# A planner's cost table for TensorE set to other numbers

## The chip, the cores and the metric

The kernel runs on one core of one Trainium2 chip. The metric is the device time of one execution in microseconds (us); smaller is better. The engines are named as in the profile: PE is TensorE (matrix products and transposes), DVE is VectorE, ACT is ScalarE, POOL is GpSimd, SP is the engine that here issues all transfers (DMA). PEclk is the share of TensorE's full clock of 2.4 GHz that was granted; 0.5 is its lower level, 1.2 GHz.

## What is computed

One layer of a hybrid encoder on two request groups that share the weights: 528 rows of a new stream (16 meta rows and 512 frames) and 64 rows of a running one. Cut to what matters:

```
h = rms_norm(x, pre_gain)                       # 592 rows of 2048
g_q, g_k, g_v, g_z, g_r, s_q, s_k, s_v, s_z, m_gla, m_sb = split(h @ w_in)
log_a = log_sigmoid(g_r @ w_a2 + b_a) / 16      # decays
o_gla, s_new = gla_recurrence(g_q, g_k, g_v, log_a, s0)        # 4 heads, key width 128, value width 256
y_gla = (rms_norm(o_gla) * silu(g_z)) @ w_up_gla
o_sb  = stick_breaking_attention(s_q, s_k, s_v)                # 8 heads of 128, with 1024 cached keys
y_sb  = (o_sb * silu(s_z)) @ w_up_sb
y = x + rms_norm((sigmoid(m_gla) * y_gla + sigmoid(m_sb) * y_sb) @ w_o, post_gain)
```

## The kernel before

**The products.** All large products are done at about full fp32 precision with three products each: weights and activations are split into a high and a low part, and `passes` runs high times high, high times low and low times high. The weight product is also cut by one level of Strassen's scheme (`strassen`): a column block of 256 is a *pair* of 14 *units*, which use the seven operand blocks W11, W22, S3, S1, S2, W12 and S4 in this order, two units each. A unit is four 128x128 weight blocks, so twelve products on PE, of 288 or 296 columns each. The operand tiles of these blocks are called `h0h`, `h0l` (W11) to `h6h`, `h6l`; S1 is `h3`, S3 `h5` and S4 `h2`. There are 44 such pairs for `w_in`, then the units of the two up projections, the linear rest and `w_o`, 786 in all.

**What a unit needs.** SP loads the weights into `raw` (three buffers). DVE forms the sums S1 to S4 in place (`raw<-raw`). ACT casts a quarter of `raw` to the high part `whi`, DVE subtracts to get the low part `wlo`. `whi` and `wlo` are rings of four tiles, and `convert` (from line 322) starts a unit only when the unit four places earlier has been done on PE. When S2 is done, DVE adds its bank to `u` twice (`u<-u,b`), and the second sum uses the bank of S1. S4 is accumulated onto the bank of S1, so its first unit must wait for these adds; its products are `b<-h2h,whi`.

**The side work.** Beside the units run the decays (a scan whose results `nu` go out as `d_cs`), four heads of the gated recurrence (`gla_head`: loads of `k`, `cs` and `q`; products of `q` and `k`; four levels in which DVE, ACT and POOL make `x` from `cs`, `q` and `k` and PE multiplies it into a bank that DVE copies by a mask into `sc`; turned values `cs<-b`; state products `b<-cs,k`) and eight stick-breaking heads (with the sums `L` on POOL).

**What sets the order.** Each of these is a Python generator. `Plan.run` repeatedly takes the stream whose next step is due first, and it emits that step; so the program text, and with it the order on every in-order engine and on SP, comes out of the plan's own clock. `Plan.note` advances this clock: an instruction begins when its engine is free and its inputs are ready, and lasts for what `Plan.cost` says. Nothing in the table is seen by the chip. All instructions go through one helper, so that every row of the profile shows line L197; the rows are told apart by their tiles.

Of the kernel before, what the change touches and what calls it, by code (L numbers as in the profile page):

```python
# [9 lines left out]
F32 = mybir.dt.float32  # L10
# [68 lines left out]
class Plan:  # L79
# [19 lines left out]
    def cost(self, eng, name, out, ins, summed):  # L99
        n = 1  # L100
        for x in out.shape[1:]:
            n *= x
        psum = any(x.tensor.name in self.psum for x in ins)
        if eng == "pe":
            dt = ins[0].dtype
            if dt == BF16:
                return 0.107
            if name == "transpose":
                return 0.053 if n < 64 else 0.11
            return max(0.214, n * 1.67e-3) if dt == F32 else max(0.11, n * 0.42e-3) + 0.003  # L110
        if eng == "act":
            return (0.055 if psum else 0.095) + (0.09 if summed or len(ins) > 1 else 0.0) + n * 0.83e-3
        if eng == "dve":
            if name == "tensor_scalar" and not psum:
                return 0.07 + n * 0.52e-3
            return 0.07 + n * (6.3e-3 if name == "reciprocal" else 1.04e-3)
        if name == "memset":
            return 0.04 + n * 0.83e-3
        return 0.15 + n * (3.5e-3 if name == "tensor_scalar" else 2.1e-3)
# [1854 lines left out]
```

## Time and profile before

| | |
|---|---|
| median of 3 runs | 1744.12 us (1739.87 to 1744.42) |
| profiled execution | 1741.68 us, of it 1739.9 us span |
| mean granted TensorE clock | 0.986 |
| PE, DVE, ACT, POOL busy | 96%, 72%, 49%, 10% of the span |
| instructions in the span | 31534, of them 12089 products on PE |

The busy shares are averages over the whole span: the stretch up to 700 us has the decays and the recurrence as side work, the one up to about 1100 us the stick-breaking heads, and the rest is almost products alone. A row of the timeline gives the start, the duration and, in brackets, how long the engine had been idle and what released it. Products overlap in the pipeline, so that each is listed as longer than the distance between two starts.

### The profile page before, as it was taken

The page shows a single profiled execution, that of the slowest core. Times are in us where ns is not written, and L with a number is a line of the kernel's source. Part 1 is how long each engine was busy: PE and PEld are TensorE (multiplying, and loading weights), DVE is VectorE, ACT ScalarE, POOL GpSimd, SP SyncE. Part 2 cuts the span into 40 slices and gives each one's busy share as a digit, 9 for nine tenths or more (in the row PEclk, how much of TensorE's full clock was granted, in tenths as well). Part 3 has the DMA queues.
Part 4 walks back from the last instruction along what each step waited for, and adds up shares of the span by engine and source line. Part 5 has one row for each costly group of instructions (what it writes and reads, how often), then busy time and mean ns, then how long its engine had stood idle before and what let it go on. Part 6 is the DMA issues. An engine that isn't in the chain of part 4 may idle for free.

```text
span 1739.9 us, 31534 instructions
## 1 busy us (share of the span) xinstructions
PE 1670.2 (96%) x12089; PEld 1610.1 (93%) x12089; DVE 1250.6 (72%) x2081; ACT 853.8 (49%) x1759; POOL 182.2 (10%) x293
## 2 busy tenths in 40 slices
PE   4998999899999999999999999999999999999997
PEld 2798999889999998999999999999999999999996
DVE  5877878887987886886677667666766435687777
ACT  5554444344454353455565555555544323355554
POOL 2100220120130021021020011111000000000000
PEclk9999999999999999999999999999999999999998
DMA  7144234344444424455445544554447444423336
GB/s 189 37 140 131 77 107 139 101 116 123 122 117 128 132 60 119 126 163 159 133 137 152 148 140 117 158 158 126 128 138 218 143 142 124 122 79 103 104 80 218
DMA packets 323904, 224.14 MB, mean 129 GB/s; under 512 B 17436, under 2 KB 293432, under 8 KB 322584
## 3 DMA queue, kind: packets, MB, share of 16 engines
q1 hardware_dynamic: 323016, 219.49, 44.3%
q10 hardware_dynamic: 736, 2.62, 0.4%
q8 instruction: 95, 1.56, 0.4%
q14 instruction: 57, 0.47, 0.1%
HBM read 179.17 MB, written 42.90 MB: 128 GB/s over the span
## 4 chain that ended last, share of the span: by engine, by line
PE 89%; DVE 5%; DMA 2%; ACT 1%; issue 1%; POOL 1%; SPq 0%; DVEq 0%; ACTq 0%; POOLq 0%
PE b L197 89%; DVE wlo L197 2%; DVE raw L197 1%; DMA xt<-in_x_sample 1%; ACT whi L197 0%; DVE u L197 0%; DVE t L197 0%; DMA q<-d_gq 0%; POOL h5l L197 0%; DMA xt<-in_x_prompt 0%; DVE x L197 0%; POOL L L197 0%; DVE out L197 0%; SPq L197 0%; DMA raw<-in_w_in 0%
## 5 line engine op out<-in xcount | busy, mean ns | idle before, releaser
L197 ACT CAST whi<-raw 128x512 fp32r<-128x512 f32 x786 | 482.0, 620 | 627.6 <-PE b L197 516.2
L197 DVE TENSOR_TENSOR wlo<-raw,whi 128x512 fp32r<-128x512 f32 x786 | 552.6, 713 | 303.9 <-ACT whi L197 293.7
L197 DVE TENSOR_TENSOR raw<-raw 128x1024 f32<-128x1024 f32 (+1 forms) x232 | 259.5, 1121 | 6.0
L197 PE MATMUL b<-m,whi 128*128 128x288 f32 x912 | 183.5, 296 | 0.0
L197 PEld LDWEIGHTS b<-m,whi 128*128 128x128 f32 x912 | 146.1, 188 | 0.0
L197 PE MATMUL b<-h0h,whi 128*128 128x288 f32 (+1 forms) x480 | 134.3, 304 | 1.3 <-ACT whi L197 1.3
L197 PE MATMUL b<-m,wlo 128*128 128x288 f32 x456 | 134.2, 294 | 0.0
L197 PE MATMUL b<-h6h,whi 128*128 128x288 f32 (+1 forms) x480 | 133.8, 303 | 0.0
L197 PE MATMUL b<-h6l,whi 128*128 128x288 f32 (+1 forms) x480 | 131.5, 298 | 1.9 <-DVE h6l L197 1.8
L197 PE MATMUL b<-h4h,whi 128*128 128x288 f32 (+1 forms) x480 | 133.0, 302 | 0.0
L197 PE MATMUL b<-h1h,whi 128*128 128x288 f32 (+1 forms) x480 | 132.1, 300 | 0.0
L197 PE MATMUL b<-h0l,whi 128*128 128x288 f32 (+1 forms) x480 | 131.5, 299 | 0.0
L197 PE MATMUL b<-h4l,whi 128*128 128x288 f32 (+1 forms) x480 | 130.4, 296 | 0.0
L197 PE MATMUL b<-h1l,whi 128*128 128x288 f32 (+1 forms) x480 | 130.3, 296 | 0.0
L197 PE MATMUL b<-h0h,wlo 128*128 128x288 f32 (+1 forms) x416 | 124.4, 299 | 1.5 <-DVE wlo L197 1.5
L197 PE MATMUL b<-h4h,wlo 128*128 128x288 f32 (+1 forms) x416 | 123.2, 296 | 1.6 <-DVE wlo L197 1.6
L197 PE MATMUL b<-h1h,wlo 128*128 128x288 f32 (+1 forms) x416 | 123.3, 296 | 0.8 <-DVE wlo L197 0.8
L197 PE MATMUL b<-h6h,wlo 128*128 128x288 f32 (+1 forms) x416 | 123.7, 297 | 0.0
L197 PE MATMUL b<-h2h,whi 128*128 128x288 f32 (+1 forms) x352 | 112.5, 319 | 10.7 <-DVE u L197 10.7
L197 PE MATMUL b<-h2h,wlo 128*128 128x288 f32 (+1 forms) x352 | 107.5, 305 | 1.0 <-DVE wlo L197 1.0
L197 PE MATMUL b<-h5h,whi 128*128 128x288 f32 (+1 forms) x352 | 108.5, 308 | 0.0
L197 PE MATMUL b<-h3h,whi 128*128 128x288 f32 (+1 forms) x352 | 107.9, 307 | 0.0
(263 smaller groups left out, 4084.8 us busy)
## 6 DMA issues: line engine op xcount, KB each, us to landing
raw<-in_w_in SPq DMA_DIRECT2D x176, 512.0 KB, 4.5
raw<-in_w_o SPq DMA_DIRECT2D x32, 512.0 KB, 4.0
raw<-in_w_up_gla SPq DMA_DIRECT2D x16, 512.0 KB, 5.3
raw<-in_w_up_sb SPq DMA_DIRECT2D x16, 512.0 KB, 4.7
d_mg<-out SPq DMA_DIRECT2D x16, 288.0 KB, 2.2
d_ms<-out SPq DMA_DIRECT2D x16, 288.0 KB, 2.1
gate<-d_mg SPq DMA_DIRECT2D x16, 288.0 KB, 5.4
gate<-d_ms SPq DMA_DIRECT2D x16, 288.0 KB, 5.5
```

Of the source, the lines that this page charges most:

```text
L197: return real(*args, **kw)
```

## The change

Three lines of the cost table for PE are given other numbers: a product of two-byte operands, a transpose, a product in four passes (plain fp32), and a wide product (the three-product scheme). For 288 columns the last goes from 0.124 to 0.1325 us, a four-pass product of 128 columns or fewer from 0.214 to 0.224 or a little more, a two-byte product from 0.107 to 0.056; a short transpose from 0.053 to 0.11.

```diff
             if dt == BF16:
-                return 0.107
+                return 0.056
             if name == "transpose":
-                return 0.053 if n < 64 else 0.11
-            return max(0.214, n * 1.67e-3) if dt == F32 else max(0.11, n * 0.42e-3) + 0.003
+                return 0.11
+            return max(0.224, n * 1.67e-3 + 4e-3) if dt == F32 else max(0.112, n * 0.4167e-3 + 0.0125)
```

No instruction is added or taken away; the instructions of all engines are put in another order. Three places are shown.

On DVE, around the `u` adds of pair 8 (the units 121 to 128 of the program). Before, from the next-to-last `wlo` group of the pair on:

```order
L197 TENSOR_TENSOR wlo<-raw,whi 128x512
L197 TENSOR_TENSOR raw<-raw 128x1024
L197 TENSOR_TENSOR x_3265<-x_3265,q 128x10x32
L197 TENSOR_TENSOR wlo<-raw,whi 128x512 x4
L197 TENSOR_TENSOR raw<-raw 128x1024 x2
L197 TENSOR_TENSOR u<-u,b_3273 128x296
L197 TENSOR_TENSOR u<-u,b_3222 128x296
L197 TENSOR_TENSOR out<-u,b_3182 128x8
L197 TENSOR_TENSOR out<-u,b_3182 128x288
```

After, up to the same adds:

```order
L197 TENSOR_TENSOR x_3196<-x_3196,q 128x10x32
L197 TENSOR_TENSOR wlo<-raw,whi 128x512 x2
L197 TENSOR_TENSOR raw<-raw 128x1024
L197 TENSOR_TENSOR out<-out,b_3202 128x8
L197 TENSOR_TENSOR out<-out,b_3202 128x288
L197 TENSOR_TENSOR wlo<-raw,whi 128x512
L197 COPY_PREDICATED sc<-lmask,b_3191 128x512
L197 TENSOR_TENSOR u<-u,b_3271 128x296
L197 TENSOR_TENSOR u<-u,b_3233 128x296
```

Before, four `wlo`, the last two of them for the next pair, and two `raw` sums in a row stand ahead of the two `u` adds; after, one `wlo` and one masked copy stand right ahead of them, and the last `raw` sum three rows earlier.

On DVE, in head 0 of the recurrence, around the `wlo` of the units 75 to 78. Before (here the first `wlo` is that of unit 76):

```order
L197 COPY_PREDICATED sc<-lmask,b_2151 128x80x4
L197 TENSOR_TENSOR wlo<-raw,whi 128x512
L197 TENSOR_TENSOR x_2197<-cs 128x320 x2
L197 TENSOR_TENSOR wlo<-raw,whi 128x512 x2
L197 TENSOR_TENSOR x_2197<-x_2197,q 128x320
L197 TENSOR_TENSOR wlo<-raw,whi 128x512 x2
L197 TENSOR_TENSOR out<-out,b_2218 128x288
L197 TENSOR_TENSOR wlo<-raw,whi 128x512
L197 COPY_PREDICATED sc<-lmask,b_2275 128x320
```

After (here the first `wlo` is that of unit 76, the last row holds those of units 77 and 78; `b_2242` holds the products of `x_2180`, which PE runs right before unit 77):

```order
L197 TENSOR_TENSOR wlo<-raw,whi 128x512
L197 SCALAR_TENSOR_TENSOR e<-out 128x288
L197 COPY_PREDICATED sc<-lmask,b_2142 128x80x4
L197 TENSOR_TENSOR x_2180<-cs 128x320 x2
L197 SCALAR_TENSOR_TENSOR e<-out,e 128x288
L197 TENSOR_TENSOR x_2180<-x_2180,q 128x320
L197 COPY_PREDICATED sc<-lmask,b_2242 128x320
L197 TENSOR_TENSOR out<-out,b_2213 128x288
L197 TENSOR_TENSOR x_2251<-cs 128x512
L197 TENSOR_TENSOR x_2251<-cs 128x128
L197 TENSOR_TENSOR wlo<-raw,whi 128x512 x2
```

Before, the masked copies, the sums of `cs` and the products with `q` stand singly between seven `wlo`; after, ten operations stand between two.

On SP, the loads for head 0. Before:

```order
L197 DMA lmask<-in_consts 128x512
L197 DMA raw<-in_w_in 128x8x128 x2
L197 DMA k<-d_gk_907 128x528
L197 DMA k<-d_gk_907 128x64
L197 DMA cs<-d_cs_1007 128x640
L197 DMA q<-d_gq_1227 128x512
L197 DMA q<-d_gq_1227 128x64
```

After:

```order
L197 DMA lmask<-in_consts 128x512
L197 DMA k<-d_gk_977 128x528
L197 DMA k<-d_gk_977 128x64
L197 DMA cs<-d_cs_1063 128x640
L197 DMA q<-d_gq_1222 128x512
L197 DMA q<-d_gq_1222 128x64
L197 DMA raw<-in_w_in 128x8x128 x2
```

Before, a pair of weight loads stands between `lmask` and the loads of `k`, `cs` and `q`; after, it stands behind them. On PE the first product of head 0 that needs `q` stands behind unit 58 instead of unit 55, and on DVE the last scan of the decays behind the `wlo` of unit 57 instead of 53. On all engines the stick-breaking heads stand beside the units 331 to 530 instead of 345 to 579.

## Rows read from the trace of the kernel before

**Rows 1.** The page, busy time and share of the span, by engine.
```profile
PE 1670.2 (96%) x12089; PEld 1610.1 (93%) x12089; DVE 1250.6 (72%) x2081; ACT 853.8 (49%) x1759; POOL 182.2 (10%) x293
```

**Rows 2.** Table by stretch: length, busy us (count) of each engine, clock, DMA.
```profile
core 0: us, PE busy (x) PEld busy (x) DVE busy (x) ACT busy (x) POOL busy (x), PEclk, DMA share, GB/s
0.00:100.00 100.00, 70.93 (x397) 55.31 (x398) 72.08 (x157) 55.52 (x132) 18.00 (x23) 0.97 0.46 115
100.00:700.00 600.00, 570.69 (x4123) 555.05 (x4122) 480.33 (x790) 280.10 (x551) 92.25 (x124) 0.97 0.40 115
700.00:1700.00 1000.00, 997.61 (x7384) 974.99 (x7383) 670.00 (x1069) 502.28 (x1016) 69.00 (x145) 1.00 0.47 134
1700.00:1740.00 40.00, 30.97 (x191) 24.72 (x189) 28.15 (x69) 15.93 (x60) 2.90 (x1) 0.88 0.65 237
1400.00:1500.00 100.00, 100.00 (x752) 100.00 (x752) 49.26 (x80) 33.34 (x52) 0.00 (x0) 1.00 0.45 130
```

**Rows 3.** PE's waits: total us, times, longest us.
```profile
PE b L197 <- DVE u L197: 10.7, 3, 4.2
...
PE b L197 <- DVE cs L197: 5.8, 4, 2.7
...
PE b L197 <- DMA q<-d_gq: 5.5, 1, 5.5
...
PE b L197 <- DVE wlo L197: 4.9, 6, 1.6
...
PE b L197 <- DVE x L197: 1.3, 3, 0.6
...
PE b L197 <- POOL L L197: 1.2, 3, 0.4
```

**Rows 4.** Table by stretch, the six stretches behind PE's long waits; first and sum.
```profile
170.65:174.30 3.65, 3.65 (x16) 3.65 (x17) 2.04 (x5) 1.71 (x3) 1.19 (x1) 0.50 0.02 4
...
sum 25.15, PE 25.13 PEld 25.15 DVE 15.47 ACT 8.90 POOL 6.66; mean PE 4.19 PEld 4.19 DVE 2.58 ACT 1.48 POOL 1.11
```

**Rows 5.** Timeline near pair 8: start us, us, row; in brackets idle before, releaser.
```profile
314.49 2.48 DVE L197 TENSOR_TENSOR wlo<-raw,whi 128x512 fp32r<-128x512 f32 x4
...
317.00 2.48 DVE L197 TENSOR_TENSOR raw<-raw 128x1024 f32<-128x1024 f32 x2
...
319.40 0.95 DVE L197 TENSOR_TENSOR u<-u,b 128x296 f32<-128x296 f32 x2
...
320.50 0.59 PE L197 MATMUL b<-h2h,whi 128*128 128x296 f32 x1 [4.22 <-DVE u L197]
```

**Rows 6.** Timeline of SP's DMA issues ahead of head 0, and PE's wait.
```profile
162.16 1.00 SPq L197 DMA_DIRECT2D raw<-in_w_in  x2
...
165.42 0.84 SPq L197 DMA_DIRECT2D q<-d_gq  x2
...
170.65 0.98 PE L197 MATMUL b<-q,k 128*128 128x128 f32 x3 [5.54 <-DMA q<-d_gq]
```

**Rows 7.** Timeline at head 1's state products.
```profile
383.31 0.38 PE L197 MATMUL b<-ident,x 128*128 128x128 f32 x2
...
386.40 1.44 PE L197 MATMUL b<-cs,k 128*128 128x128 f32 x5 [2.71 <-DVE cs L197]
```

**Rows 8.** Timeline, DVE's small operations of head 0.
```profile
203.97 0.51 DVE L197 COPY_PREDICATED sc<-lmask,b 128x320 f32<-128x320 int32 x1
...
220.92 0.45 DVE L197 TENSOR_TENSOR out<-out,b 128x288 f32<-128x288 f32 x1
...
223.12 0.92 DVE L197 TENSOR_TENSOR x<-cs 128x512 f32<-128x512 f32 x2
```

**Rows 9.** Timeline at 365; one tile's operations (min/median/max ns): wlo, then GpSimd's x, q.
```profile
365.01 4.83 DVE L197 TENSOR_TENSOR wlo<-raw,whi 128x512 fp32r<-128x512 f32 x3 [0.27 <-ACT whi L197]
...
365.30 2.03 POOL L197 TENSOR_TENSOR x<-x,k 128x640 f32<-128x640 f32 x1
...
L197 DVE TENSOR_TENSOR wlo<-raw,whi x468: 673/692/1289, 699.5 to 1699.9; 128x512 fp32r<-128x512 f32 x156
...
L197 POOL TENSOR_TENSOR x<-x,k x32: 735/1037/2026, 171.8 to 651.1; 128x320 f32<-128x320 f32 x24, 128x256 f32<-128x256 f32 x4, 128x640 f32<-128x640 f32 x4
...
L197 POOL TENSOR_TENSOR q<-q,x x4: 2012/2280/2557, 226.8 to 653.1; 128x640 f32<-128x640 f32 x4
```

## The prediction, made before the changed kernel was run

> **What bounds the kernel now.** The page comes first. PE is busy 96% of the span and DVE, the next, 72% [rows 1]. So PE's products are the floor, the change removes none of them, and only the time in which PE waits or runs slowly can move. The second view asks where that is. The table by stretch shows 570.69 us of PE work in the 600 us from 100 to 700, and 997.61 us in the 1000 us from 700 to 1700 [rows 2]: 29.3 us of idle time lie in the first stretch, 2.4 in the second. The first 100 us (29.1 idle) and the last 40 (9.0) are waits for the input, the first norms and the last results; the order of the kernel before and of the changed one is the same there up to the tenth unit and from unit 602 on, so they stay. The third view names the waits. Within 100 to 700 the large ones are DVE's `u` adds (10.7 us, 3 times), `cs` copies (5.8, 4 times), one load of `q` (5.5) and DVE's `wlo` (4.9, 6 times) [rows 3]. The fourth view is the granted clock: right behind each of the six waits of over 2.5 us PE was granted the lower of its two levels, 1.2 GHz, for 3 to 5.7 us; at 170.65 to 174.30 the clock is 0.50 and PE is full all the while [rows 4]. No wait of 1.6 us or less is followed by such a stretch. The six stretches sum to 25.15 us, 25.13 of them busy, so half of that, 12.6 us, is lost besides. Waits and slow stretches between 100 and 700 thus cost some 42 us, and that is the stake.
>
> **The numbers of the table.** From 1400 to 1500 PE is never idle and starts 752 products of 288 columns [rows 2]: 133.0 ns each. The old table says 124 ns, the new one 132.5. A unit of twelve products is then 1.59 us in the plan against 1.49 before, where the trace has 1.60. The plan thought PE 7% faster than it is, so every piece of side work that it set by PE's time stood late against PE's true place; now more side work, by the same 7%, is put beside each unit.
> The Trainium skill ("TensorE: Matmul & The Clock Gate", section Back-to-back issue gap) gives N/2.4 + 2.5 ns for an isolated product at the full clock and says itself that a stream of loads and products departs from it. For 288 columns that is 122.5 ns, near the old entry; by it the new table would be the wrong one, and the packing of rival B would follow. The 133.0 ns above decide against it.
>
> **The u adds: -10.7 us.** The operand tiles `whi` and `wlo` form a ring of four, so the tile of a unit can be filled only when the unit four places before it is done. DVE works in order. At pair 8 the two `u` adds stand behind four `wlo` and two `raw` sums, and the last of these `wlo` belongs to the second unit of the next pair; its ring place comes free only when PE has finished the last unit ahead of S4, which is the unit that needs `u`. Hence PE has nothing left to do while DVE works off one `wlo`, two `raw` sums (2.48 us) and the adds (0.95): a wait of 4.22 us [rows 5]. Of 44 pairs exactly three (4, 8 and 18, counted from 0) have the adds behind two `wlo` of the next pair, and exactly these three wait. In the changed order the adds stand at latest behind S4's own second `wlo`, two units earlier, and behind one `raw` sum at most in the places named. Places as good as that never waited before. So all 10.7 us go; I bound it by -8.
>
> **The load of q: -3 us.** Before head 0 SP issues a pair of weight loads at 162.16, then `k`, `cs` and, at 165.42, `q`; PE's first product of `q` and `k` starts at 170.65 after 5.54 us [rows 6]. In the changed order that weight pair stands behind `q`, and PE has three more units (4.8 us) ahead of the product. Against that the last scan, whose result SP must write out ahead of these loads, moves back by four `wlo`, some 6.4 us. I take 2.5 us as left, between 0 and 5.5.
>
> **The cs copies: -2.6 us.** In heads 1 and 3 the copy of the turned values stood behind a `wlo` whose place came free only with the unit right before the state products; at 383.31 the last turns run, and the products `b<-cs,k` start at 386.40, 2.71 us late [rows 7]. Head 3's copy now stands two or three units earlier, so its 2.64 us go. Head 1's large copy moves forward too, but the small one, needed by the fifth state product, still stands behind the same `wlo`: its wait stays. Between 0 and -5.4.
>
> **A new tight place: +4 us.** In head 0 the changed order puts ten DVE operations between the `wlo` of units 76 and 77. One of them, the masked copy into `sc`, reads five `x` products that PE runs right before unit 77. Behind these products DVE still has the copy (0.51 us), an `out` add (0.45) and two `cs` sums (0.92) [rows 8], and then the `wlo` (0.69 in the median, [rows 9]): 2.6 us, and by my estimate 0.4 of hand-over (a `u` add that ends at 320.35 lets PE start at 320.50, [rows 5]), in which PE has nothing. Ahead of them GpSimd's product (0.74 to 2.03 us, [rows 9]) may make the `x` late as well, by 0 to 3. Together 4, between 1 and 6. Before, these operations stood between seven `wlo`.
>
> **Other side work: +3.5 us.** The eight stick-breaking heads now run in units 331 to 530, where they took 345 to 579. Three waits for `L` of at most 0.4 us (1.2 in all) [rows 3] show how near they are; I take four more, 1.5 us, between 0 and 5. In heads 2 and 3 `x` products may come late as three did (1.3 us, [rows 3]): 2, between 0 and 4.
>
> **The slow stretches: -6.3 us.** Waits of over 2.5 us should be left at unit 77 and in head 1; at q and at one more place the chance is even. That makes three stretches of 25.15/6/2 = 2.1 us lost each, where there were six: 6.3 of 12.6 stay. Between -12.6 and +3.
>
> **Sum:** -10.7 - 3 - 2.6 + 4 + 3.5 - 6.3 = -15.1 against the profiled execution's 1741.7 us, that is 1726.6. That execution was 2.4 below the median of the runs, 1744.1; on the median's footing it is 1729.
>
> **Rivals.** A, no change: the waits only move. DVE has 480 us of work in the 600 us of the first stretch [rows 2], its bursts are longer than the three units' lead that a ring of four allows, and a burst taken from one pair meets PE at another: 30 us of waits stay 30, time 1740 to 1748. For it speaks the new place at unit 77; against it that every large wait of before has one cause, a copy or add behind a `wlo` too far ahead, and that just one such place is left by the changed order.
> B, slower: the plan now books PE rightly but not DVE and GpSimd. Three `wlo` took 4.83 us while GpSimd ran its 640-wide product, where the median of one is 0.69 [rows 9], so 2.8 us that no entry holds. With 7% more side work a unit, the `wlo` behind such a burst arrive after PE has used up its lead. There are eight bursts of that size (four `x<-x,k` and four `q<-q,x`); if five of them end in a new wait of 2.8 us with a slow stretch of 2.1, that is +24, and the sum -15 + 24 = +9, some 1753. Three such waits (15/4.9) eat up the gain; from four on, (15 + 5)/4.9, the kernel is slower than can be missed. For it speaks the row; against it that before, these bursts met PE with a `wlo` wait of 1.6 at most.
> The Trainium skill ("GPSIMD Engine Reference", section Specifications) says that GpSimd shares its SBUF interfaces with VectorE and contends with DVE instructions of two SBUF inputs, which `wlo` is. By that rule the packing has a cost that the table leaves out, and the row above agrees.
> C: the order hardly reaches PE, since the first stretch's waits are hidden behind something else; the time then stays at 1744. Little speaks for it, as each wait shows one releaser.
>
> **How the numbers follow.** My forecast has 0.68, A 0.15, B 0.13, C 0.04. A measurement of this kernel tells apart about 0.3%, 5.2 us. The forecast's own range is from 1715 (most of the bounds on the good side) to 1738. Below 1739 counts as faster: 0.68. A and C fall within 0.3%: 0.19. B is slower: 0.13. The range from 1715 to 1748 leaves out B's upper half and more, and a few in a hundred below.
>
> **What would show it.** In the changed profile the waits for `u` are under 1 us in sum; the wait for `q` is below 5.5; one `cs` wait of over 2 us stays, near 386; a wait of 3 us or so on `wlo` or `whi` appears some 1.6 us times 76 units in, near 205; the stretch from 100 to 700 has under 20 us of idle time and about three stretches at 0.5 instead of six; from 700 on PE stays above 99%. The forecast is wrong if `u` waits are found elsewhere, if `wlo` waits between 200 and 700 sum to over 15 us, or if the stick-breaking part (700 to 1100) shows more than 5 us of idle time.

## The result, and the profile after

The changed kernel takes 1730.59 us in the median of 7 runs (1724.02 to 1735.68), the kernel before 1742.2 us (1737.65 to 1744.42) in 7 runs beside it: a ratio of 0.9933, with a 95% interval of 0.991 to 0.9956. A later set of six runs of the changed kernel (e4 below) has a median of 1727.88 us and a ratio of 0.9922 (0.991 to 0.9934). The forecast was 1729 us.

The profiled execution took 1724.02 us, 17.7 us less than that of before, and was the fastest of the seven; the medians lie 12 to 15 us apart. The page's line on busy time and the table by stretch, to be set beside [rows 1, 2]:

```profile
PE 1660.1 (96%) x12089; PEld 1599.9 (93%) x12089; DVE 1247.8 (72%) x2081; ACT 853.7 (50%) x1759; POOL 183.0 (11%) x293
```
```profile
0.00:100.00 100.00, 69.37 (x405) 54.23 (x406) 71.58 (x156) 55.25 (x132) 18.01 (x23) 0.98 0.45 115
100.00:700.00 600.00, 582.45 (x4287) 567.40 (x4286) 500.44 (x823) 292.37 (x572) 93.05 (x126) 1.00 0.43 121
700.00:1700.00 1000.00, 994.56 (x7354) 971.89 (x7353) 662.40 (x1070) 500.28 (x1036) 69.02 (x144) 1.00 0.47 135
```

The counts of instructions are the same. PE's busy time falls from 1670.2 to 1660.1 us although it runs the same 12089 products: most of these 10 us are products that no longer run at the lower clock (the mean granted clock is 0.994, where it was 0.986). In the 600 us from 100 to 700 the idle time of PE falls from 29.3 to 17.6 us, and DVE gets 500 us of work done where it did 480. From 700 to 1700 the idle time rises from 2.4 to 5.4.

PE's waits over the whole execution, beside [rows 3] (total, times, longest):

```profile
...
PE b L197 <- DVE x L197: 5.2, 6, 1.4
PE b L197 <- DVE wlo L197: 4.0, 5, 1.5
PE b L197 <- DMA x<-d_gv: 3.7, 2, 2.2
PE b L197 <- POOL L L197: 3.2, 4, 1.6
PE b L197 <- ACT whi L197: 2.7, 2, 1.4
PE b L197 <- DMA q<-d_gq: 2.6, 1, 2.6
...
PE b L197 <- DVE cs L197: 1.8, 1, 1.8
```

No row for `u` is left. Between 100 and 700 us the list has no wait above 2.6 us; it has more small ones, above all for `x`, `x<-d_gv` and `L`.

The new tight place at unit 77, in the timeline:

```profile
212.38 0.87 DVE L197 COPY_PREDICATED sc<-lmask,b 128x320 f32<-128x320 int32 x1 [2.30 <-PE b L197]
...
213.72 0.40 PE L197 MATMUL b<-h3h,whi 128*128 128x288 f32 x1 [1.38 <-ACT whi L197]
...
214.25 1.29 DVE L197 TENSOR_TENSOR wlo<-raw,whi 128x512 fp32r<-128x512 f32 x2
...
214.99 0.40 PE L197 MATMUL b<-h3h,wlo 128*128 128x288 f32 x1 [0.73 <-DVE wlo L197]
```

It is where the forecast put it, and costs 2.1 us, by another way in part: 1.38 us are for `whi`, which the forecast had not named and which ACT casts behind its own side work; only the 0.73 us after it are for `wlo`, behind the masked copy, the add and the sums. DVE had itself been idle for 2.30 us ahead of the copy, which reads PE's products. Head 1's small `cs` copy, the one wait of this kind that was to stay:

```profile
371.89 0.68 DVE L197 TENSOR_TENSOR wlo<-raw,whi 128x512 fp32r<-128x512 f32 x1
...
373.30 0.28 DVE L197 COPY cs<-b 128x128 f32<-128x128 f32 x1
...
373.73 0.46 PE L197 MATMUL b<-cs,k 64*128 64x128 f32 x2 [1.85 <-DVE cs L197]
```

The clock, read as in [rows 4]: the stretch behind the wait for `q`, and that behind the `cs` wait:

```profile
172.40:175.70 3.30, 3.30 (x16) 3.30 (x15) 1.81 (x4) 1.62 (x5) 1.99 (x2) 0.50 0.00 0
...
373.80:377.20 3.40, 3.40 (x25) 3.28 (x26) 2.53 (x7) 1.67 (x4) 0.81 (x1) 1.00 0.28 101
```

Only the first runs at 1.2 GHz. It is the one slow stretch between 100 and 700 in this execution, where before had six.

### The profile page after: what moved, and what is told of

Read it like the earlier page. It is cut to its first block, busy times and chain, and to the rows that moved or that the text cites. A ratio compares the mean times of both kernels' runs of the same rounds, so it can differ in the third digit from the quotient of the medians.

```text
span 1722.2 us, 31529 instructions
## 1 busy us (share of the span) xinstructions
PE 1660.1 (96%) x12089; PEld 1599.9 (93%) x12089; DVE 1247.8 (72%) x2081; ACT 853.7 (50%) x1759; POOL 183.0 (11%) x293
## 3 DMA queue, kind: packets, MB, share of 16 engines
q8 instruction: 95, 1.56, 0.4%
## 4 chain that ended last, share of the span: by engine, by line
PE 87%; DVE 5%; DMA 3%; issue 2%; ACT 2%; POOL 1%; SPq 0%; DVEq 0%; ACTq 0%; POOLq 0%
PE b L197 87%; DVE wlo L197 1%; DVE x L197 1%; DMA xt<-in_x_sample 1%; DMA x<-d_gv 1%; DVE raw L197 0%; DMA stage<-d_og 0%; ACT whi L197 0%; POOL L L197 0%; DVE t L197 0%; POOL x L197 0%; POOL h5l L197 0%; DMA xt<-in_x_prompt 0%; SPq L197 0%; ACT x L197 0%
## 5 line engine op out<-in xcount | busy, mean ns | idle before, releaser
L197 DVE TENSOR_TENSOR wlo<-raw,whi 128x512 fp32r<-128x512 f32 x786 | 544.8, 705 | 275.1 <-ACT whi L197 266.7
L197 PE MATMUL b<-h2h,whi 128*128 128x288 f32 (+1 forms) x352 | 106.6, 303 | 0.0
L197 PE MATMUL b<-h3h,wlo 128*128 128x288 f32 (+1 forms) x352 | 104.6, 297 | 1.1 <-DVE wlo L197 1.1
```

Of the source, the lines that this page charges most:

```text
L197: return real(*args, **kw)
```

## The experiments

### One part of the table at a time

**e1** keeps the new wide entry alone, **e2** the other three alone.

```diff
 e1, against before:
-            return max(0.214, n * 1.67e-3) if dt == F32 else max(0.11, n * 0.42e-3) + 0.003
+            return max(0.214, n * 1.67e-3) if dt == F32 else max(0.112, n * 0.4167e-3 + 0.0125)
 e2, against the changed kernel:
-            return max(0.224, n * 1.67e-3 + 4e-3) if dt == F32 else max(0.112, n * 0.4167e-3 + 0.0125)
+            return max(0.224, n * 1.67e-3 + 4e-3) if dt == F32 else max(0.11, n * 0.42e-3) + 0.003
```

> Only the entry of the wide product has the new number; the other three lines are as before. In the order that comes out no pair has its u adds behind the wlo of the next pair's second unit, and no cs copy stands behind a wlo whose ring place comes free only with the unit right before the state products. Theory 1 (the old entry let DVE's wlo run ahead of the adds and copies that PE needs; the new wide entry alone cures it): no u wait, cs waits under 1 us in sum, at most two slow stretches between 100 and 700, time 1724 to 1733. Theory 2 (the order is a matter of chance, any other table would have done as much or as little): u and cs waits turn up again somewhere, time anywhere from 1730 to 1750.

> The wide entry is as before; two-byte products, transposes and four-pass products have the new numbers. The order has the u adds behind two wlo of the next pair in pairs 4 and 18 (not in 8), and no cs copy in the worst place. Theory 1: two u waits of 2.5 to 4 us, each with a slow stretch, nothing at pair 8, cs waits under 1 us: 3 to 4 of 10.7 us of u waits and 5 of cs waits saved, some 6 us of slow stretches; time 1730 to 1738, slower than with the wide entry alone by 4 to 10. Theory 2: as e1, within 3 us of it. If the small entries carried the change, it would reach 1727 to 1731.

Measured: e1 1741.54 us in the median, ratio to before 0.9995 (0.9983 to 1.0007); e2 1744.12 us, 1.001 (0.9997 to 1.0024). Neither part alone gains anything, so theory 1 failed in both; the times lie in theory 2's ranges, e2 2.6 us above e1. In e1 the places are as foretold, with no `u` wait and no `cs` wait. These were 16.5 us before, but PE's idle time from 100 to 700 falls only from 29.3 to 25.9 us, with five slow stretches for six, and behind 700 us new waits (5.1 us of idle time up to 1700, where before had 2.4) and a slow stretch at 882 take up most of that: PE now waits for something else. (That `u` or `cs` waits would turn up again, as theory 2 had it, did not come true.) Its largest rows of waits from 100 to 700:

```profile
PE b L197 <- DMA x<-d_gv: 13.1, 4, 6.9
PE b L197 <- DVE x L197: 3.4, 5, 1.4
PE b L197 <- POOL x L197: 3.1, 2, 2.6
```

The longest of them, at head 3, in the timeline:

```profile
657.22 4.93 POOL L197 TENSOR_TENSOR q<-q,x 128x640 f32<-128x640 f32 x1
...
662.17 1.76 SPq L197 DMA_DIRECT2D x<-d_gv  x4
...
665.09 0.69 PE L197 MATMUL b<-ident,x 128*128 128x128 f32 x2 [6.88 <-DMA x<-d_gv]
```

The load of the values needs the buffer that GpSimd's product `q<-q,x` reads last. That product took 4.93 us here, while in the changed kernel the four of them took 1.56 to 2.0 us. DVE ran `raw` sums and `wlo` beside it. The transposes that need the load stood ready on PE for 6.88 us. The slow product accounts for some 3 us of this wait (an estimate, from 4.93 against 2.0 us). Two further waits of this row, 2.69 and 2.88 us, came where that product took 2.55 and 1.78 us; what makes them long was not looked into.

In e2 the `u` adds stand behind two `wlo` of the next pair in the pairs 4 and 18, and there the waits are, 2.60 and 3.85 us, as in before. The place tells where PE waits in these two orders. The other two rows below are waits that the expectation did not name, and they bring the time back to that of before:

```profile
PE b L197 <- DMA x<-d_gv: 10.1, 5, 3.3
PE b L197 <- DVE u L197: 6.9, 3, 3.8
...
PE b L197 <- ACT whi L197: 4.6, 1, 4.6
```

### The old table with a rule against the bad place

**e3** keeps the table of before and holds back the next pair's `wlo` and `raw` sums until the `u` adds are out.

```diff
-            yield lambda: state["hi"] > state["conv"]
+            yield lambda: state["hi"] > state["conv"] and units[state["conv"]].get("held", lambda: True)()
...
+        past = ahead.get("in") if kind == "in" else None
+        ahead[kind] = box
+        def held():
+            return past is None or ("S2", "out") in past
...
-                    preps.append((lambda x="a" if to == "S3" else "b": loaded(x), n_conv, ...
+                    preps.append((lambda x="a" if to == "S3" else "b": loaded(x) and held(), n_conv, ...
```

> The table is that of before, all old numbers; but the plan may not emit a wlo or a raw sum of a pair before the u adds of the pair ahead of it are out. The order then has no u add behind another pair's wlo, and no cs copy in the worst place. Theory 1: no u wait, cs waits under 1.5 us, at most two slow stretches, so some 13 us of waits and 8 to 12 of slow clock less, against a few new waits elsewhere: 1724 to 1734 with the wrong numbers in the table. Theory 2 (waits only move, or what counts is that the plan knows PE's pace): within 5 us of before, 1738 to 1747.

Measured: 1738.33 us, 0.9975 (0.9964 to 0.9986). No `u` wait is left; of the 8 to 18 us that this was to bring, 4 came, a time in theory 2's range. The plan had put everything else in another order too, and waits for `q` (6.2 us), `whi` (4.5), `x<-d_gv` (4.2) and `wlo` (3.8) stand in the list; the `cs` waits are 2.5 us, where under 1.5 were expected.

### The changed kernel once more

> The changed kernel once more, for a second profile. Its seven runs lay between 1724 and 1736 at mean clocks of 0.994 to 0.990, and the one profiled was the fastest. Theory: the same waits stand in it to within some tenths of a us, and what varies is how many of the waits of 1.5 to 2.6 us are followed by a slow stretch (one between 100 and 1200 in the first profile); a run that is 6 us longer has two to four more of them. Rival: the waits themselves vary, transfers above all, by 5 us or more in sum. Median 1727 to 1733.

Measured: 1727.88 us in the median of 6. The waits between 100 and 1700 stand at the same instructions as in the first profile; the largest difference is 0.7 us, at `q`. The profiled execution is 4.3 us longer, and between 100 and 700 it has the lower clock behind three waits instead of one, at 3.3, 2.1 and 1.85 us of waiting (`q`, unit 77, `cs` in head 1):

```profile
173.30:176.60 3.30, 3.30 (x16) 3.30 (x16) 2.33 (x5) 2.05 (x4) 1.58 (x2) 0.51 0.00 0
217.60:220.90 3.30, 3.30 (x16) 3.30 (x15) 3.30 (x4) 0.62 (x1) 2.44 (x3) 0.50 0.89 235
378.10:381.40 3.30, 3.30 (x16) 3.30 (x15) 1.80 (x5) 0.62 (x1) 0.80 (x1) 0.51 0.32 113
```

So the same wait of 1.85 us was followed by a slow stretch in one execution and not in the other. Two stretches of 3.4 us at half speed are 3.4 of the 4.3 us. The mean clock of the first seven runs goes from 0.994 in the fastest to 0.990 in the slowest. By these two numbers the slow clock makes up at most 7 of the 11.7 us between them (an estimate: 0.4% of 1724 us); four runs at 0.990 still lie between 1730.6 and 1735.7 us.

### Other numbers for the wide entry

Four tables more: **e5** and **e6** are the changed one with its wide entry 2% up and 2% down, **e8** 7% up; **e7** is the table of before with its wide entry 7% lower still.

```diff
-            return ... max(0.112, n * 0.4167e-3 + 0.0125)
+            return ... max(0.112, n * 0.4167e-3 + 0.0125) * 1.02
 e6: * 0.98, e8: * 1.07, and e7:
-            return ... max(0.11, n * 0.42e-3) + 0.003
+            return ... (max(0.11, n * 0.42e-3) + 0.003) * 0.93
```

> The changed kernel with its wide entry 2% higher (0.1352 us for 288 columns where the trace has 0.133). The order is quite another one: u adds behind the next pair's second wlo once (pair 13), all else about as good. Theory 2 (the planner's order reacts to any number; what an order costs is the chance of where its waits fall): away from the changed kernel's 1729 by 4 to 15 us, 1733 to 1744, one u wait of 2.5 to 4 us and new waits for x<-d_gv or whi. Theory 3 (it is the nearness of the numbers to the trace that pays): 1726 to 1732, since 2% is little against the 7% that was corrected.

> The changed kernel with its wide entry 2% lower (0.1299 us for 288 columns). All four heads of the recurrence stand some 14 to 20 units later in it; no u add is in the worst place. Theory 2: between 1728 and 1744, unlike the changed kernel's list of waits; theory 3: 1726 to 1732.

> The table of before with its wide entry 7% lower still (0.115 us for 288 columns, 13% under the trace). Three pairs have their u adds behind the next pair's second wlo and a dozen behind its first. Theory 3: the plan is further off, so that waits grow in step: 1750 to 1760. Theory 2: about as before, 1737 to 1749, since three such waits are what before had.

> The changed kernel with its wide entry 7% higher (0.1418 us for 288 columns, 6.6% above the trace). No u add in the worst place, no cs copy either. Theory 3: an error of the old size on the other side puts too much side work beside a unit, so wlo waits: 1738 to 1750. Theory 2: anywhere between 1727 and 1743. A plan that takes PE for too slow and so errs on the safe side would give 1725 to 1732.

The orders of e5 and e7 do not compute the layer: all instructions are there, but the two outputs y are wrong, so some instruction stands too early or too late, and a wait that a right order needs may be missing. Which one was not looked for. These two times carry less weight.

| wide entry, 288 columns | other three | ratio to before (95%) |
|---|---|---|
| 0.115 us (e7) | old | 1.033 (1.0309 to 1.0351) |
| 0.124 (before) | old | 1 |
| 0.124 (e2) | new | 1.001 (0.9997 to 1.0024) |
| 0.130 (e6) | new | 1.0096 (1.0082 to 1.011) |
| 0.1325 (changed, e4) | new | 0.9922 (0.991 to 0.9934) |
| 0.1325 (e1) | old | 0.9995 (0.9983 to 1.0007) |
| 0.135 (e5) | new | 0.9958 (0.9944 to 0.9971) |
| 0.142 (e8) | new | 0.9973 (0.9963 to 0.9982) |

Two things stand in this table. A change of 2% in one number moves the time by up to 30 us, from 1728 to 1758 (e6): the planner turns a small change of a cost into quite another order, and what that order costs was not to be read off the size of the change (theory 2). And none of the tables with a wide entry of 0.130 us or less is faster than before, while three of the four with 0.1325 or more are (the trace has 0.133); one of the three is e5.

The forecasts did poorly one by one. e5 (1735.4 us) and e8 (1736.9) fell into the ranges of theory 2, but e6 (1758.5) and e7 (1802.0) lie above every range named. Nor did the place foretell the `u` wait here: e5 has the adds in the worst place once, and its `u` wait was 1.0 us; e6 has none there, and waits 2.2 us for `u` once. In e7, 13% below the trace, side work is left over at the end and waits stand everywhere:

```profile
PE b L197 <- DVE wlo L197: 11.5, 7, 4.0
PE b L197 <- DVE u L197: 11.0, 3, 4.2
PE b L197 <- ACT h0h L197: 10.8, 1, 10.8
```

The 10.8 us are the operands of the up projection, which the last stick-breaking heads deliver too late, at 1371 us. Its order has three pairs in the worst place, and three `u` waits.

### One place moved and nothing else

In e1 to e8 the whole order changes with the number. To try a single wait, the choices of `Plan.run` were written down for the kernel before and replayed, with some of them moved:

```diff
-            e = min(able, key=self.due)
+            e = next(x for x in able if x["id"] == ord(PICKS[step]) - 48)
+            step += 1
```

(The helper stands at L285 in these kernels.) **e9** moves the `u` adds of the pairs 4, 8 and 18. On DVE this is, at pair 8 (at pair 4 the adds also pass one `x` row, at pair 18 an `out` add goes with them; all else keeps its order, GpSimd's part of `x` at pair 4 apart, which stands one place later):

```diff
-TENSOR_TENSOR wlo<-raw,whi 128x512 x4
-TENSOR_TENSOR raw<-raw 128x1024 x2
+TENSOR_TENSOR wlo<-raw,whi 128x512 x2
 TENSOR_TENSOR u<-u,b_3273 128x296
 TENSOR_TENSOR u<-u,b_3222 128x296
 TENSOR_TENSOR out<-u,b_3182 128x8
 TENSOR_TENSOR out<-u,b_3182 128x288
+TENSOR_TENSOR wlo<-raw,whi 128x512 x2
+TENSOR_TENSOR raw<-raw 128x1024 x2
```

> The order of before, written down step by step and replayed, so that no clock of the plan chooses; at pairs 4, 8 and 18 alone the u adds are moved ahead of the next pair's two wlo and two raw sums. Nothing else moves on any engine. Theory 1 (these waits are PE's own loss and go when the place is mended): the three u waits (10.7 us) and the slow stretches at 203, 320 and 605 (15 us at half speed) go, so 1742.5 - 10.7 - 7.4 = 1724, between 1721 and 1729. Theory 2a (the waits only move, since DVE has as much to do as before): wlo or raw come as much later, 1738 to 1744.

Measured: 1743.24 us against 1743.17, ratio 1.0002 (0.9994 to 1.0011). Theory 1 failed outright: the three waits are gone, and nothing is gained. The time is theory 2a's, though what comes late is neither `wlo` nor `raw`. The timeline at pair 8 shows where they went:

```profile
315.63 1.28 DVE L285 TENSOR_TENSOR wlo<-raw,whi 128x512 fp32r<-128x512 f32 x2
316.84 0.95 DVE L285 TENSOR_TENSOR u<-u,b 128x296 f32<-128x296 f32 x2
...
317.93 0.37 PE L285 MATMUL b<-h2h,whi 128*128 128x296 f32 x1 [0.50 <-DVE u L285]
...
319.58 2.49 DVE L285 TENSOR_TENSOR raw<-raw 128x1024 f32<-128x1024 f32 x2
321.99 1.75 DVE L285 COPY_PREDICATED sc<-lmask,b 128x512 f32<-128x512 int32 x3
...
326.79 1.01 DVE L285 TENSOR_TENSOR x<-x,q 128x320 f32<-128x320 f32 x1
...
327.94 0.87 PE L285 MATMUL b<-x 128*128 128x64 f32 x3 [4.90 <-DVE x L285]
```

Call a product of PE that must wait for a result of DVE a gate. PE waits 3.7 us less at the `u` gate, runs its three units, and then stands at the next gate, the `x` products of the recurrence, for 4.90 us. DVE had the same work ahead of that gate in both orders. The row that ends it stands in the trace of before at

```profile
325.63 1.02 DVE L197 TENSOR_TENSOR x<-x,q 128x320 f32<-128x320 f32 x1
```

From the first `wlo` (314.49 in [rows 5], 315.63 in e9) to this row it takes 11.14 us before and 11.16 in e9, of which DVE idles 0.7 in either; in before the wait at `u` had hidden the second one. With the 0.50 us left at `u` and the `x` waits at 202, 211 and 615 us (1.68, 1.30 and 2.00) the sum over the three places is 10.4 us, where the `u` waits were 10.7. The slow stretches behind the waits moved with them, from 203, 320 and 605 us to 203, 326 and 616.

**e12** moves the two `raw` sums of the same three pairs behind these `x` rows as well (and at pair 4 leaves `u` behind the `x` row that e9 had overtaken).

> The order of before replayed; at pairs 4, 8 and 18 the u adds stand ahead of the next pair's wlo as in e9, and the next pair's two raw sums (2.48 us of DVE time) now stand behind the next x<-x,q rows, where e9 had left them ahead. In e9 the u waits had passed to those x (1.68, 1.30, 4.90 and 2.00 us). Theory 4 (PE waits at the next gate that needs DVE, and what counts is how much DVE work stands ahead of each gate): the x waits shrink by up to 2.5 each, to about 3.5 us in sum, with one or two slow stretches fewer: 1733 to 1737. Theory 2a (DVE's load over the stretch binds wherever its rows stand): the raw sums are late in turn and whi of the next pair's S3 waits, 1740 to 1745.

Measured: 1737.64 us, 0.9971 (0.9959 to 0.9983). The gate at pair 8 now reads

```profile
322.45 1.01 DVE L285 TENSOR_TENSOR x<-x,q 128x320 f32<-128x320 f32 x1
...
323.61 1.08 PE L285 MATMUL b<-x 128*128 128x64 f32 x8 [2.39 <-DVE x L285]
```

2.5 us less, which is the 2.48 us of the two `raw` sums; at pair 18 the wait shrank only from 2.00 to 1.81, and at pair 4 one of 1.77 stayed. So the rule came out to the number at one place of three, and the sum over the three is 6.0 us where theory 4 had 3.5. The gain of 5 us is on the side of theory 4, a little short of its range, and no wait for the next pair's `whi` came up.

**e10** adds to e9 the large `cs` copies of heads 1 and 3.

> As e9, and the large cs copies of heads 1 and 3 one or two wlo earlier. Theory 1: two more waits (2.7 and 2.6 us) and their slow stretches (6.7 us at half speed) go, 8 to 9 us less than e9: 1713 to 1720, less than the changed kernel. If the small cs copy of the same heads becomes the one that is late, half of it: 1717 to 1724. Theory 2a: as before, 1738 to 1744.

Measured: 1739.67 us, 0.9972 (0.9962 to 0.9982): 3.6 us less than e9. The time is theory 2a's; the range of the second guess, 1717 to 1724, started from a gain in e9 that did not come. What the second guess said of the waits held: those of 2.74 and 2.64 us became 1.69 and 1.65 at the last state product, which needs the small copy.

**e11** replays the changed kernel and mends its two worst places of this kind: `whi` and `wlo` of the units 77 and 78 go ahead of the masked copy, head 1's small `cs` copy ahead of two `wlo`.

> The changed kernel's order replayed, with two places mended: whi and wlo of units 77 and 78 ahead of the masked copy of the five x products, and head 1's small cs copy ahead of the wlo of units 159 and 160. Theory 1: the waits of 2.1 and 1.85 us go, with the slow stretches that follow them in some runs (two of 3.4 us in e4): 1729 - 4 - 2 = 1723, between 1720 and 1726. If the masked copy, now later, is waited for in its turn: within 2 us of 1729.

Measured: 1724.59 us (1723.75 to 1725.74), ratio to the kernel before 0.9894 (0.9878 to 0.9909), the fastest median of all, of four runs and in theory 1's range; the changed kernel itself did not run beside it. The `cs` wait is gone; at unit 77 the 2.1 us became 1.5 us at the next `x` products, as at the gates above.

## Why the prediction held, and where it did not

**The sum.** Forecast were -15.1 us against the profiled execution; the two profiles of the changed kernel have -17.7 and -13.3. The steps by their own rows:

| step | forecast | profile after |
|---|---|---|
| u adds | -10.7 | -10.7, no such wait left |
| load of q | -3 | -2.9 (5.5 to 2.6) |
| cs copies | -2.6 | -4.0 (5.8 to 1.8), head 1's stays |
| unit 77 | +4 | +2.1 |
| x products, L | +3.5 | +5.9 (x 1.3 to 5.2, L 1.2 to 3.2) |
| slow stretches | -6.3, three left | one left (-10.9); three left in the second profile (-7.5) |

For the last line one stretch is 3.4 us at half speed, so 1.7 us lost, against the 12.6 us of before. The three that the second profile shows are those that were named: `q`, unit 77, head 1. The time is the sum of terms that came out smaller and larger than forecast: unit 77 was half its size, the `x` products and `L` over half as large again.

**The step that failed** is the reasoning under the first line, "So all 10.7 us go", and with it the argument against rival A, that every large wait has one cause and goes when its place is mended. e9 mends exactly these places and gains 0.0%: the waits pass to the next gate behind them on DVE's list. So the row of -10.7 came true, but not for the reason given, and that the time came out too is in part luck: the same reasoning, with `u` and `cs` waits gone, would have forecast a gain for e1, which has none. Rival A was right on a single place. Its mechanism was the one that I had given it, DVE's burst against PE's lead; what I had against it, the place behind the `wlo`, tells where PE waits, not what it can save. e12 shows the other half at pair 8, where 2.48 us less of DVE work ahead of a gate shortened its wait by 2.5 us; at the pairs 4 and 18 the waits shrank by less.

**Why the changed order gains all the same.** By rows, it is the stretch from 100 to 700: 11.8 us less of waits and 10.7 less lost at the lower clock, against some 6 us more behind 700. Beside e1, which has the same wide entry, it has 9.4 us less of waits for `x<-d_gv`, and one slow stretch (three in the second profile) where e1 has five. Why this order meets fewer late gates is not shown: DVE idles 99.6 us of the 600 instead of 119.7, but that follows already from PE getting further in them. That this comes from the numbers being nearer to the trace is only partly shown. For it: no table with a wide entry of 0.130 us or less gains, and the one furthest below costs 3.3% (e7, whose order is not a right one). Against it: the right wide entry alone gains nothing (e1), 2% more or less gives 0.9958 (e5, likewise) or 1.0096, and the old numbers with a rule gain 0.25% (e3). The likeliest reading is a trend with a scatter of about 1% from order to order; how much of the 0.7% is the one and how much the other stays open. What in the new order of the small entries removes e1's 13 us of waits for `x<-d_gv` was not tried by itself.

**Rival B** was right on the price and wrong on what PE pays of it. In the changed kernel GpSimd's large products took 1.56 to 2.0 us, and DVE paid: four `wlo` beside two of them took 4.99 us at 349.46, where four took 2.48 in [rows 5]. Yet no wait of over 0.4 us for `wlo` stands behind them. In e1 the price fell on GpSimd once, and came to PE not through `wlo`, but through a buffer that the slow product held and a load that came late. Which of the two pays is seen in one `raw` sum beside `q<-q,x`, in the changed kernel (first two rows) and in e1:

```profile
625.63 1.57 POOL L197 TENSOR_TENSOR q<-q,x 128x640 f32<-128x640 f32 x1
625.69 2.60 DVE L197 TENSOR_TENSOR raw<-raw 128x1024 f32<-128x1024 f32 x1
...
658.93 1.21 DVE L197 TENSOR_TENSOR raw<-raw 128x1024 f32<-128x1024 f32 x1
```

In e1 the product took 4.93 us and the sum its usual 1.2. The Trainium skill ("GPSIMD Engine Reference", section Specifications) has the contention of GpSimd with DVE instructions of two SBUF inputs; the `raw` sum at 2.60 and at 1.21 us agrees with it. In both cases the one that started first was not held up: in the changed kernel the product, by 0.06 us; in e1 a `raw` sum that started at 657.20, ahead of the product at 657.22, and the three `wlo` and `raw` rows behind it went first as well. Two cases are not yet a rule.

**What was not in the sum**: 1.0 us more for `x<-d_gv`, 1.6 less for `wlo` at other places than unit 77, and behind 1300 us 2.3 us more at `h6l` and at the end, with one more slow stretch behind the first (1.7 us). I had called that part unchanged since its order is; the waits were not. With these the rows add up to -17.1 and -13.1, against the -17.7 and -13.3 measured.

## What to carry to other kernels

A wait in a trace names the first gate at which a busy engine is late, not the time to be had by mending it: ask which gate on the same engine's list comes next, and how much of that engine's work stands ahead of it; only work taken from ahead of both gates can shorten the path (2.5 us at pair 8 in e12, less at the other two places). With a planner that picks by its own clock, every number reorders the whole program, so a gain from a better number must be judged against neighbours of that number (here 2% up and down) before it is credited to the number's truth. Freeze the order and move single rows if a cause is to be tested, or a last per cent to be had: that gave the fastest kernel here, 1724.6 us.

## What the runs showed of the hardware that was not expected

- The same GpSimd product of 128x640 elements (`q<-q,x`) took between 1.54 (e7) and 4.93 us (e1). Beside one of 1.57 us a DVE `raw` sum took 2.60 us, beside the one of 4.93 us 1.21. The second case reached PE, through a transfer.
- Waits of 1.85 and 2.1 us were followed by 3.4 us at 1.2 GHz in one execution and not in another of the same program. The length of a wait alone does not tell: waits of 2.88 us (e1, at 374) and 2.73 (e12, at 385) were followed by none, waits of 1.05 (e8, at 196) and 1.49 (e11, at 214) by one. What does was not tested.
- A few waits carry most of what PE loses beside its products: before, six waits of 2.6 to 5.5 us are 21.6 of the 29.3 us of idle time between 100 and 700, and all the 12.6 us lost at the lower clock stand behind them.
